# Retention's output projection in a two-layer trunk: another order of the seven Strassen products, other places for sums and splits

## The chip, the cores and the metric

The kernel runs on one core of a Trainium2 chip. The metric is the device time of one execution in microseconds (us). The engines are named as the profile names them: PE (TensorE matmul), PEld (its weight load), DVE (VectorE), ACT (ScalarE), POOL (GpSimd), SP (SyncE, which issues most DMAs). Before the change three runs gave 1338.38, 1340.61 and 1341.14 us, median 1340.61.

## The reference

Two layers, each x + f(x): a retention layer (4 heads, keys of 256, values of 512, chunks of 128 tokens, a recurrent state), then sliding-window attention. The prompt has 1024 tokens and 8 more tokens are decoded. All is float32. What the change touches is the end of the retention layer:

```python
o, S = retention_scan(q, k, v, S0)                 # (B, L, 4 heads, 512)
o = rmsnorm(o, g_out.reshape(RET_HEADS, RET_DV)).reshape(B, L, RET_V)   # 2048 wide
o = o * jax.nn.silu(gate)
return x + o @ w_out, S.astype(S0.dtype)           # w_out is 2048 x 1024
```

## The kernel before, in words

A float32 product is made as three passes over rounded parts: with x = xh + xl and w = wh + wl (h the rounded value, l what is left), PE adds wh·xh, wh·xl and wl·xh. So each operand needs a copy that rounds (ACT, the "hi" part) and a subtraction (DVE or POOL, the "lo" part).

**Retention steps.** 32 steps, one for each head and chunk. Each leaves a gated output block. Blocks of the first half of the 2048 rows (part a of the projection) stay in SBUF as `hold`; those of the second half (part b) go to DRAM, `osc`.

**Strassen.** Part a and part b each multiply 1024 tokens by a 1024 x 1024 half of w_out, as 2 x 2 blocks. Seven products replace eight: activations come as raw blocks (B11, B21, B22) or as sums of them (T1 to T4), weights as raw blocks (A11, A12, A22) or sums (S1 to S4, tiles `s`; `raw` is the loaded weight). A weight sum S2 is made from S1, and S4 from S2. Activation blocks are rounded to `oxh` by `ox_hi` (L881, ACT) and `oxl` by `ox_lo` (L885); the decoded tokens' two columns for each block are split by `dec_split` (L895, L896) and summed by `dec_sums` (L901). Sums of `hold` blocks are `sum_op` (L1052, DVE).

**Sets and slots.** A set is one part and one of four column groups q: sets 0 to 3 are part a, sets 4 to 7 part b. A set has seven products in two token halves t, 14 slots of 12 matmuls (L1127 to L1129). In part a the last four products also take the residual x by two transposes for each slot (L1132), from tiles `xr` that a DMA loads (L1180) and, for the last, POOL subtracts from one another (`res_diff`, L1183). Weights are summed on POOL (`w_sum`, L209 to L218) and split by `w_hi` (L238, ACT) and `w_lo` (L243, DVE).

The order is A11, S2, S1, A12, S3, S4, A22. Each product is written to one of three PSUM banks for each t or added to what stands there: A12 is added to the bank of A11, S4 to that of S1, and S3 and A22 to that of S2. Since the combination needs what stood in a bank between its products, the bank is read first (`o_evac`, L1148 to L1164: ACT for A11, and for A12 in part a; DVE else) into `evp`, `evx`, `evc`, `evw`. So A12 waits until A11's bank is read, and A22 until S3's is, with two products and one product between them.

**What sets the order.** A planner (`Table`) lists the slots with assumed times; `when(t, ...)` puts a piece of work before the slot that is due at t, `later(n, ...)` behind slot n. Each engine executes its instructions in the order in which they are written, so a late operand delays all that stands behind the instruction that waits for it.

**Part b's activations.** During sets 0 to 3 the raw blocks are loaded from DRAM into one ring of five tiles `ob` (L1112), summed (L1354, two sums of each group of four on DVE, two on POOL) and stored again. From set 3 on, all 28 blocks are loaded once more into the same ring and split into `oxh` and `oxl`, the lo parts alternately on DVE and POOL.

**Out of a set.** `out_a` (L1203) stores part a's result; `out_b` adds it to part b's (`pa_add` L1195, L1211), squares it for the next norm and stores it. In set 7 `a_split` (L1252, L1253) and `kvs_conv` (L1410, L1411) prepare attention's operands and weights.

Of the kernel before, what the change touches and what calls it, by code (L numbers as in the profile page):

```python
# [7 lines left out]
F32 = mybir.dt.float32  # L8
# [65 lines left out]
def _trunk(ctx, tc, nc, a):  # L74
# [129 lines left out]
    def w_sum(s, name, sub, part=0):  # L204
        sh = [128, 512 // s.fw, s.fw]
        wq, nb = (s.pool(), 1) if s.kind == "o" else (wq_, 2)
        if name == "S2" and part == 0:
            t = s.sum["S1", sub] = wq.tile(sh, F32, tag="s1", bufs=nb, name="s1")
            pool.tensor_tensor(t, quad(s, 1, 0, sub), quad(s, 1, 1, sub), ADD)  # L209
        elif name == "S2":  # L210
            t = s.sum["S2", sub] = wq.tile(sh, F32, tag="s2", bufs=nb, name="s2")
            pool.tensor_tensor(t, s.sum["S1", sub], quad(s, 0, 0, sub), SUB)  # L212
        elif name == "S3":
            t = s.sum["S3", sub] = wq.tile(sh, F32, tag="s1", bufs=nb, name="s3")
            pool.tensor_tensor(t, quad(s, 0, 0, sub), quad(s, 1, 0, sub), SUB)
# [4 lines left out]
    def wop_tile(s, sh, nm):  # L220
        if s.kind == "o":
            return s.pool().tile(sh, F32R, tag="wop", bufs=6, name=nm)
# [642 lines left out]
    ORD7 = (B11, T2, T1, B21, T3, B22, T4)  # L865
# [25 lines left out]
    def dec_split(x):  # L891
# [3 lines left out]
        dve.tensor_copy(h, src)  # L895
        dve.tensor_tensor(l, src, h.bitcast(F32), SUB)  # L896

    def dec_sums():
        a_, b_, c_, d_ = dec_blocks(0)
        for out, x, y in ((a_, c_, a_), (c_, d_, c_), (d_, d_, a_), (b_, b_, d_)):  # L900
            dve.tensor_tensor(out, x, y, SUB)  # L901
# [149 lines left out]
    def sum_op(out, x, y):  # L1051
        dve.tensor_tensor(out, x, y, SUB)  # L1052
# [14 lines left out]
    plan_builds(6, 30)  # L1067
# [40 lines left out]
    KEYS = (("c", 0, 0), ("w", 1, 1), ("x", 0, 1), ("p", 1, 0))  # L1108
# [29 lines left out]
    def o_raw(s, j):  # L1138
        t = s.pool().tile([128, 4, 256], F32, tag="raw", bufs=2, name="raw")
# [4 lines left out]
    def o_evac(s, j, t):  # L1144
        c = s.c
        b0, b1, b2 = [s.bk[i, t][:, 0:258] if (i, t) in s.bk else None for i in range(3)]
        if j == 0:
            act(o_out(s, "p", t), b0, AF.Copy)  # L1148
        elif j == 1:
            dve.tensor_tensor(c["p", t], b1, c["p", t], ADD)  # L1150
        elif j == 2:
            dve.tensor_tensor(o_out(s, "x", t), b2, c["p", t], ADD)
        elif j == 3 and s.part == 0:
            act(o_out(s, "c", t), b0, AF.Copy)
        elif j == 3:
            dve.tensor_tensor(o_out(s, "c", t), b0, s.pa["c"][:, t, :], ADD)
        elif j == 4 and s.part and s.q:
            dve.tensor_tensor(c["w", t], b1, c["w", t], ADD)  # L1158
        elif j == 4:
            dve.tensor_tensor(o_out(s, "w", t), b1, c["x", t], ADD)  # L1160
        elif j == 5:
            dve.tensor_tensor(c["x", t], b2, c["x", t], ADD)
        else:
            dve.tensor_tensor(c["p", t], b1, c["p", t], ADD)  # L1164
# [12 lines left out]
    def res_load(s, key, i, par):  # L1177
        r = s.res[key] = sg[0].tile([128, 4, 128], F32, tag="xr", bufs=4, name="xr")
# [11 lines left out]
    def pa_add(s, key):  # L1190
        if key == "w":
            for t in range(2):
                o_out(s, "w", t)
        src = both(s, "x" if key == "w" else key)
        pool.tensor_tensor(both(s, key), src, s.pa[key], ADD)  # L1195
# [10 lines left out]
    def out_b(s, key, i, par):  # L1206
# [3 lines left out]
        if key != "c" and s.q == 0:  # L1210
            dve.tensor_tensor(r, r, s.pa[key], ADD)  # L1211
# [4 lines left out]
        if s.q == 3:  # L1216
# [5 lines left out]
            dve.scalar_tensor_tensor(alo, pr, gk, af, MUL, SUB)  # L1222
        if s.q == 0 and key in "cw":
# [5 lines left out]
        for t in range(2):  # L1229
            soon_dma(xscr[ft, :, 512 * t:512 * t + 512].rearrange("p (c r x) -> r p c x", r=2, x=128)[par], pr[:, t])  # L1230
# [11 lines left out]
    def a_load(k, par, tile_=lambda: ob[0].tile([128, 4, 128], F32, tag="ob", bufs=5, name="ar")):  # L1242
# [21 lines left out]
    def o_slot(s, j, t):  # L1264
        name, x, b, first = SEQ7[j]
# [1230 lines left out]
```

## Time and profile before

| | us |
|---|---|
| runs (median of three) | 1340.61 |
| profiled execution | 1336.95 |
| its span, first to last instruction | 1335.1 |
| retention steps | 551.5 to 706.6 |
| projection, sets 0 to 7 | 708.29 to 894.20 |
| PE busy in the projection's 185.91 us | 175.70 |
| DVE, ACT, POOL busy there | 127.36, 76.35, 130.96 |

A line of the trace has a start, a duration, the engine and line, the operation with output and input tiles, and in brackets the idle time before it with what ended it. A line of waits has engine, line, what it waited for, us in total, number of times, the longest. A line of a table of windows has the window and its length, then for each engine its busy time and number of instructions, TensorE's granted clock, the DMA engines' busy share and GB/s. A PE that is busy in a window may still be slow inside a slot; a slot's cost is read from start to start.

### The profile page before, as it was taken

What the parts mean: (1) busy time and instruction counts of PE and PEld (TensorE: products, weight loads), DVE (VectorE), ACT (ScalarE), POOL (GpSimd) and SP (SyncE); (2) the same over time, 40 slices, a digit from 0 to 9 for tenths busy, and PEclk for the clock granted to TensorE, in tenths of its full rate; (3) what the DMA queues carried; (4) which work ended last, traced back from release to release, by engine and by line L of the source; (5) the groups of instructions that cost most, each with busy time, mean ns of one, the idle gap of its engine ahead of it and who ended that gap; (6) DMA issues with size and microseconds to landing.
All of it is one profiled execution on the core that took longest, in us unless ns stands there. A gap on an engine that the chain in (4) does not pass through costs nothing.

```text
span 1335.1 us, 26918 instructions
## 1 busy us (share of the span) xinstructions
PE 1276.3 (96%) x9613; PEld 1231.1 (92%) x9613; DVE 852.9 (64%) x1684; ACT 709.0 (53%) x1739; POOL 852.9 (64%) x1011
## 2 busy tenths in 40 slices
PE   6999999999999999899899998988999999999998
PEld 6999999999999999787689998988999999998998
DVE  6953655665666554487987567576677777778421
ACT  5522545555555664376664244345576676766321
POOL 6643555656556665378797576875688787878510
PEclk9999999999999999999999998999999999999999
DMA  6313867586667762545777987653131110113532
GB/s 223 103 50 109 241 190 237 171 257 202 189 209 215 224 194 89 190 159 188 211 232 218 324 273 243 176 171 96 45 93 51 33 60 25 46 29 108 186 95 77
DMA packets 217306, 207.93 MB, mean 156 GB/s; under 512 B 19348, under 2 KB 185228, under 8 KB 217156
## 3 DMA queue, kind: packets, MB, share of 16 engines
q1 hardware_dynamic: 188848, 178.27, 43.0%
q10 hardware_dynamic: 28324, 27.94, 6.7%
q8 instruction: 76, 1.25, 0.4%
q14 instruction: 58, 0.48, 0.1%
HBM read 137.10 MB, written 70.09 MB: 155 GB/s over the span
## 4 chain that ended last, share of the span: by engine, by line
PE 67%; POOL 11%; DVE 10%; DMA 6%; issue 4%; ACT 2%; SPq 0%; POOLq 0%; ACTq 0%; DVEq 0%
PE b L359 7%; PE b L361 7%; PE b L360 7%; PE pj L1593 5%; PE pj L1594 5%; PE pj L1595 5%; PE b L353 4%; PE b L354 4%; PE b L352 4%; PE tr L104 3%; DMA ob<-osc 2%; DVE Sl L1006 1%; POOL s L2038 1%; POOL pw L1578 1%; PE S L1129 1%
## 5 line engine op out<-in xcount | busy, mean ns | idle before, releaser
L359 PE MATMUL b<-xh,woh 128*128 128x258 f32 x784 | 222.1, 283 | 0.0
L361 PE MATMUL b<-xh,wol 128*128 128x258 f32 x784 | 221.5, 283 | 0.0
L360 PE MATMUL b<-xl,woh 128*128 128x258 f32 x784 | 221.3, 282 | 0.0
L1593 PE MATMUL pj<-A_hi,pw 128*128 128x384 f32 (+1 forms) x512 | 172.5, 337 | 0.0
L1594 PE MATMUL pj<-A_lo,pw 128*128 128x384 f32 (+1 forms) x512 | 163.9, 320 | 1.0 <-POOL A_lo L1840 0.7
L1595 PE MATMUL pj<-A_hi,pw 128*128 128x384 f32 (+1 forms) x512 | 163.8, 320 | 0.0
L359 PEld LDWEIGHTS b<-xh,woh 128*128 128x128 f32 x784 | 148.1, 189 | 1.2
L360 PEld LDWEIGHTS b<-xl,woh 128*128 128x128 f32 x784 | 148.6, 190 | 0.0
L361 PEld LDWEIGHTS b<-xh,wol 128*128 128x128 f32 x784 | 148.0, 189 | 0.0
L353 PE MATMUL b<-wol,xh 128*128 128x256 f32 x448 | 126.7, 283 | 2.5 <-DVE wol L243 2.5
L352 PE MATMUL b<-woh,xh 128*128 128x256 f32 x448 | 126.5, 282 | 0.0
L354 PE MATMUL b<-woh,xl 128*128 128x256 f32 x448 | 126.3, 282 | 0.0
L243 DVE TENSOR_TENSOR wol<-s,woh 128x512 fp32r<-128x512 f32 x120 | 102.0, 855 | 18.3 <-ACT woh L238 17.6
L238 ACT ACTIVATE woh<-s 128x512 fp32r<-128x512 f32 x120 | 73.9, 623 | 71.2 <-POOL s L212 32.4
L301 POOL TENSOR_TENSOR yl<-yd,yh 128x256 fp32r<-128x256 f32 x64 | 57.0, 890 | 79.3 <-PE od L308 42.6
L243 POOL TENSOR_TENSOR wol<-raw,woh 128x512 fp32r<-128x512 f32 x52 | 68.9, 1332 | 52.1 <-ACT woh L238 51.2
L1594 PEld LDWEIGHTS pj<-A_lo,pw 128*128 128x128 f32 x512 | 96.6, 189 | 1.6 <-POOL A_lo L1840 1.0
L1127 PE MATMUL S<-oxh,woh 128*128 128x258 f32 x320 | 94.2, 294 | 3.8 <-DVE evw L1158 2.8
L1593 PEld LDWEIGHTS pj<-A_hi,pw 128*128 128x128 f32 x512 | 96.4, 188 | 0.6 <-issue 0.3
L1595 PEld LDWEIGHTS pj<-A_hi,pw 128*128 128x128 f32 x512 | 96.2, 188 | 0.0
L1129 PE MATMUL S<-oxh,wol 128*128 128x258 f32 x320 | 92.0, 287 | 3.8 <-DVE wol L243 3.8
L1128 PE MATMUL S<-oxl,woh 128*128 128x258 f32 x320 | 91.5, 286 | 0.0
(423 smaller groups left out, 4064.2 us busy)
## 6 DMA issues: line engine op xcount, KB each, us to landing
raw<-in_w_in_ret_dram ACTq DMA_DIRECT2D x44, 512.0 KB
st<-in_state_ret_dram SPq DMA_DIRECT2D x64, 256.0 KB
out_dram<-st SPq DMA_DIRECT2D x64, 256.0 KB
vb<-vscr SPq DMA_DIRECT2D x64, 128.0 KB
evp<-qks SPq DMA_DIRECT2D x32, 256.0 KB
evw<-gsc SPq DMA_DIRECT2D x32, 256.0 KB
raw<-in_w_out_ret_dram SPq DMA_DIRECT2D x16, 512.0 KB
wr<-in_w_in_swa_dram SPq DMA_DIRECT2D x14, 512.0 KB
```

The costliest lines, as they stand in the source:

```text
L243: eng.tensor_tensor(lo, src_of(s, name, sub), hi.bitcast(F32), SUB)
L352: mm(dst, xh, wh, start=a and i == 0, stop=False, skip_group_check=True)
L353: mm(dst, xh, wl, start=False, stop=False, skip_group_check=True)
L354: mm(dst, xl, wh, start=False, stop=z, skip_group_check=True)
L359: mm(dst, wh, xh, start=a, stop=False, **sg)
L360: mm(dst, wh, xl, start=False, stop=False, **sg)
L361: mm(dst, wl, xh, start=False, stop=z, **sg)
L1127: mm(dst, wh, xh, start=a, stop=False, **sg_k)
L1129: mm(dst, wl, xh, start=False, stop=z, **sg_k)
L1593: mm(ps, wh, AH(k)[:, t0:t1], start=first and k == ks[0], stop=False)
L1594: mm(ps, wh, AL(k)[:, t0:t1], start=False, stop=False)
L1595: mm(ps, wl, AH(k)[:, t0:t1], start=False, stop=last and k == ks[-1])
```

## The change

The order of products becomes A11, A12, S4, S2, S1, S3, A22, with other banks: S4 has a bank of its own, S1 takes the one of A11 and A12, and A22 is added to S3's directly after it. What was evicted as one sum for `evx` is done in two steps, the later one after S1. Sum S4 moves from POOL to DVE, in place in raw A12. The weights have one ring of six split tiles instead of two such rings used in turn, and are prepared 4.5 us before use (S4 3.9) instead of 6.5. Residual tiles are loaded 11 us ahead instead of 8 and subtracted 7 us ahead instead of 4.5.

In the retention steps, the decoded columns' work moves from steps 15 to 22 to steps 1 to 10 (its copies from DVE to ACT). Of the sixteen sums of `hold`, the last group's four and the `b` sums of all groups move behind the last step, with T1's four splits and T2's last one; of those that stay, two of three go to POOL. The projection's first slot is issued to PE ahead of the transposes of the output of the last step but one, which came before it.

For part b, the raw blocks B11 and B21 stay in SBUF from their one load (tiles `oa`, `ob`, four each, and `ot`, five, in place of one ring of five), so that 20 blocks instead of 28 are loaded for splitting. Of its sums three of four go to DVE; of its 28 splits 16 go to DVE and 12 to POOL. Squares and stores of a set's result come some slots later, and `kvs_conv` 7 us and more later.

```diff
-    ORD7 = (B11, T2, T1, B21, T3, B22, T4)
+    SEQO = (("A11", B11, 0, True), ("A12", B21, 0, False), ("S4", B22, 1, True), ("S2", T2, 2, True),
+            ("S1", T1, 0, True), ("S3", T3, 2, True), ("A22", T4, 2, False))
...
     def w_sum(s, name, sub, part=0):
+            elif name == "S4":
+                t = quad(s, 0, 1, sub)
+                dve.tensor_tensor(t, t, s.sum["S2", sub], SUB)
...
-        dve.tensor_copy(h, src)
+        act(h, src, AF.Copy)
...
-            seq_ += [(sum_op, a_, c_, a_), (sum_op, c_, d_, c_), (ox_hi, T1, j, a_), (ox_lo, T1, j, a_),
-                     (sum_op, d_, d_, a_), (ox_hi, T2, j, d_), (ox_lo, T2, j, d_), (sum_op, b_, b_, d_)]
+            if j < 3:
+                seq_ += [(sub, a_, c_, a_), (sub, c_, d_, c_), (sub, d_, d_, a_, dve)]
+            if j < 3:
+                seq_ += [(ox_hi, T2, j, d_), (ox_lo, T2, j, d_)]
...
-            th_ = max(tf - 6.5, floor + (3.2 if name != "A11" else 0.0))
+            th = first[name] - (3.9 if name == "S4" else 4.5) - (6.0 if n_ == 0 and name in ("A11", "A12", "S4") else 0.0)
...
+    a3, c3, d3 = hold[0, 6], hold[0, 7], hold[1, 7]
+    for t_, x in ((-2.0, (a3, c3, a3)), (-0.7, (c3, d3, c3)), (0.6, (d3, d3, a3))):
+        tb.when(t_, sub, *x)
+    for j in range(3, 4):
+        tb.when(2.0, late_build, T2, j, dve)
+    for j in range(4):
+        tb.when(2.7 + 1.5 * j, lambda j=j: sub(hold[1, 2 * j], hold[1, 2 * j], hold[1, 2 * j + 1]))
+        tb.when(2.4 + 0.9 * j, late_build, T1, j, (dve, pool)[j % 2])
+        tb.when(6.2 + 0.8 * j, late_build, T3, j, (dve, pool)[j % 2])
+        tb.when(9.2 + 1.1 * j, late_build, T4, j, (dve, pool)[j % 2])
...
+        for i_, (x, n_, tag) in enumerate(((B11, 0, "oa"), ("c", 2, "ot"), ("d", 3, "ot"), (B21, 1, "ob"))):
+            tb.when(t_ + 0.05 * i_, b_load, x, n_, j, tag)
+        tb.when(t_ + 5.5, b_sums, j)
+        tb.when(t3 + 5.0 + 0.8 * j, b_load, B22, 3, j, "ot")
     m = 0.0
     for n_, x in enumerate(ORD7):
         for j in range(4):
-            m = max(m + 1.1, osets[3].t0 + 2.95 * n_ + 3.0)
-            tb.when(m - 6.0, xb_load, x, j)
-            tb.when(m, xb_build, x, j)
+            m = max(m + 1.15, t3 + 2.95 * n_ + 3.0)
+            tb.when(m, xb_build, x, j, (dve, dve, pool, dve, pool, dve, pool)[(4 * n_ + j) % 7])
+            y = {B11: (T2, 5, "oa"), B21: (T1, 4, "ob"), B22: (T3, 6, "ot"), T2: (T4, 7, "oa")}.get(x)
+            if y:
+                tb.when(m + 2.0, b_load, y[0], y[1], j, y[2])
...
+        if i == len(steps) - 1:
+            tb.pe()
         at_step(b_tr, i - 1)
```

POOL's program at the opening of the projection, from the last steps' `bss` (the norm's exponent) to the first weight sum of set 1, before the change:

```order
L120 TENSOR_TENSOR bss<-bss,mhalf 128x1 x2
L215 TENSOR_TENSOR s_9883<-raw 128x512
L885 TENSOR_TENSOR oxl<-hold,oxh 128x4x128
L218 TENSOR_TENSOR s_9777<-raw,s_9777 128x512
L885 TENSOR_TENSOR oxl<-hold,oxh 128x4x128 x3
L1203 TENSOR_TENSOR evc<-evc,xd 128x2x2
L209 TENSOR_TENSOR s_10100<-raw 128x512
```

The same stretch of POOL's program now, between the last `bss` and the residual's subtraction and the sum behind it (L1068 is a sum of `hold`, L901 a split, L216 the sum S3):

```order
L120 TENSOR_TENSOR bss<-bss,mhalf 128x1
L1068 TENSOR_TENSOR hold<-hold 128x512 x2
L901 TENSOR_TENSOR oxl<-hold,oxh 128x4x128
L1068 TENSOR_TENSOR hold<-hold 128x512
L901 TENSOR_TENSOR oxl<-hold,oxh 128x4x128
L1068 TENSOR_TENSOR hold<-hold 128x512
L216 TENSOR_TENSOR s_9979<-raw 128x512
L901 TENSOR_TENSOR oxl<-hold,oxh 128x4x128
L1068 TENSOR_TENSOR hold<-hold 128x512
L1218 TENSOR_TENSOR evc<-evc,xd 128x2x2
L901 TENSOR_TENSOR oxl<-hold,oxh 128x4x128 x2
L1201 TENSOR_TENSOR xr<-xr 128x512
```

One more split of T4 and set 1's first sums follow. Ahead of the first `bss` of this piece stand two more sums of `hold`.

DVE's program about the start of set 4, before, where part b's splits (`oxl<-ob`) stand among the weight splits of A11's followers:

```order
L885 TENSOR_TENSOR oxl<-ob,oxh 128x4x128
L1164 TENSOR_TENSOR evp<-S,evp 128x258
L885 TENSOR_TENSOR oxl<-ob,oxh 128x4x128
L243 TENSOR_TENSOR wol<-s_11007,woh 128x512
L885 TENSOR_TENSOR oxl<-ob,oxh 128x4x128
L243 TENSOR_TENSOR wol<-raw,woh 128x512
L1150 TENSOR_TENSOR evp<-S,evp 128x258
```

The corresponding piece now, from set 3's last evictions (L1181) to set 4's A12 (L1171); L212 is the sum S4:

```order
L1181 TENSOR_TENSOR evp<-po,evp 128x258
L256 TENSOR_TENSOR wol<-raw,woh 128x512
L212 TENSOR_TENSOR raw<-raw,s_11027 128x4x128
L1181 TENSOR_TENSOR evp<-po,evp 128x258
L901 TENSOR_TENSOR oxl<-ob,oxh 128x4x130 x2
L256 TENSOR_TENSOR wol<-raw,woh 128x512
L1171 TENSOR_TENSOR evc<-S,pa 128x258
L901 TENSOR_TENSOR oxl<-ob,oxh 128x4x130
L256 TENSOR_TENSOR wol<-s_11027,woh 128x512
```

The splits of `ob` still stand between the weight splits; the S4 sum has joined them. What the splits read is now mostly loaded long before.

DVE's program in set 7, up to S3's evictions (evw<-S,evw, L1158), before:

```order
L243 TENSOR_TENSOR wol<-s_11883,woh 128x512
L1156 TENSOR_TENSOR evc<-S,pa 128x258
L1253 SCALAR_TENSOR_TENSOR A_lo<-ar,gcol,A_hi 128x4x128
L1156 TENSOR_TENSOR evc<-S,pa 128x258
L1222 SCALAR_TENSOR_TENSOR A_lo<-evc,gcol,A_hi 128x4x128
L243 TENSOR_TENSOR wol<-raw,woh 128x512
L1158 TENSOR_TENSOR evw<-S,evw 128x258
```

And now, up to S3's evictions in their new form (evw<-po,evw, L1179); L1175 evicts S1, L1177 is the second step of evx:

```order
L1175 TENSOR_TENSOR evw<-S,evp 128x258
L1272 SCALAR_TENSOR_TENSOR A_lo<-ar,gcol,A_hi 128x4x128
L256 TENSOR_TENSOR wol<-raw,woh 128x512
L1177 TENSOR_TENSOR evx<-S,evw 128x258
L1175 TENSOR_TENSOR evw<-S,evp 128x258
L1272 SCALAR_TENSOR_TENSOR A_lo<-ar,gcol,A_hi 128x4x128
L1177 TENSOR_TENSOR evx<-S,evw 128x258
L1179 TENSOR_TENSOR evw<-po,evw 128x258 x2
```

Fewer wide instructions stand directly ahead of S3's evictions; the one A_lo that followed A12's evictions is further ahead.

More of the change, by code (lines that the diff above doesn't have):

```diff
@@ L1264, in o_slot @@
     def o_slot(s, j, t):
[L1265 removed]
+        name, x, b, first = SEQO[j]
         n = len(tb.slots)
[L1267 removed]
+        key = KEYS.get(name)
+        done = KEYS.get({"S1": "S4", "S4": None}.get(name, name))
+        res = s.part == 0 and key
         def pe():
@@ L1328, in open_b @@
+        if s.part == 0:
+            tb.when(first["A22"] - 7.0, res_diff, s)
+        elif s.q:
+            tb.later(s.n0 + 11, pa_add, s, "p", pool)
     def open_b():
```

228 lines of the change are left out of this document (118 added, 110 removed).

## The prediction

> **What bounds the kernel now.** I read the page first, to see which engine carries the time.
>
> ```profile
> PE 1276.3 (96%) x9613; PEld 1231.1 (92%) x9613; DVE 852.9 (64%) x1684; ACT 709.0 (53%) x1739; POOL 852.9 (64%) x1011
> ```
>
> PE does, so a change that leaves its matmuls alone can win only what PE loses. Where that is in the stages touched, I read from windows cut at the starts of the eight sets:
>
> ```profile
> core 0: us, PE busy (x) PEld busy (x) DVE busy (x) ACT busy (x) POOL busy (x), PEclk, DMA share, GB/s
> 708.29:731.54 23.25, 23.25 (x200) 23.03 (x198) 18.74 (x28) 10.78 (x23) 15.41 (x13) 1.00 0.78 236
> 731.54:754.37 22.83, 22.37 (x188) 22.02 (x186) 12.78 (x21) 5.01 (x11) 13.50 (x14) 1.00 0.92 284
> 754.37:777.85 23.48, 22.41 (x188) 22.00 (x186) 12.36 (x21) 5.53 (x12) 13.64 (x13) 1.00 0.89 301
> 777.85:800.71 22.86, 22.20 (x188) 21.99 (x186) 17.50 (x22) 13.60 (x26) 15.60 (x13) 1.00 0.90 303
> 800.71:829.52 28.81, 23.81 (x172) 23.05 (x171) 20.83 (x29) 12.64 (x24) 20.82 (x18) 0.88 0.81 261
> 829.52:849.71 20.19, 20.19 (x170) 20.19 (x169) 11.78 (x21) 8.20 (x15) 14.33 (x14) 1.00 0.60 176
> 849.71:870.16 20.45, 20.43 (x170) 20.25 (x169) 13.48 (x22) 7.65 (x15) 19.15 (x19) 1.00 0.63 181
> 870.16:894.20 24.04, 21.05 (x172) 20.54 (x171) 19.90 (x24) 12.96 (x24) 18.51 (x16) 1.00 0.66 198
> ```
>
> Set 5 runs without a gap: 20.19 us for 14 slots, 1.44 a slot. That is the floor of a part-b set. Part a has two residual transposes more in eight of its slots; its floor is about 21.9, just under the 22.0 for which PEld was busy in each of sets 1 to 3, so that such a slot takes (21.9 − 6 x 1.44) / 8 = 1.66. Above the floor lie: set 0 1.3 (0.6 of it the last step's four transposes), sets 1 to 3 0.9, 1.5 and 0.9, set 4 8.6, sets 5 and 6 0.3 together, set 7 3.9. So 17.4 us in all, half of it in set 4. What ended the waits in set 4 is in the waits of 800.7 to 829.5:
>
> ```profile
> ACT oxh L881 <- DMA ob<-osc: 11.7, 8, 2.6
> DVE oxl L885 <- ACT oxh L881: 7.5, 4, 5.7
> PE S L1129 <- DVE wol L243: 3.8, 1, 3.8
> ```
>
> In set 4, ACT waits for the reloaded blocks of part b, DVE waits for ACT inside a split of theirs, and the weight split of A12 stands behind it. The granted clock fell to 0.88 with the gap. The same reading for the retention steps: windows of steps 3 to 10 and 15 to 23, then the price of what DVE has in some of them.
>
> ```profile
> 567.94:604.54 36.60, 36.60 (x203) 30.93 (x202) 30.15 (x68) 24.34 (x60) 29.62 (x35) 1.00 0.52 166
> 623.55:670.68 47.13, 39.48 (x216) 32.14 (x215) 40.83 (x90) 29.90 (x72) 36.58 (x41) 1.00 0.74 218
> ...
> L895 DVE CAST oxh<-gdec x5: 182/425/429, 637.9 to 664.9; 128x16 fp32r<-128x16 f32 x5
> L896 DVE TENSOR_TENSOR oxl<-gdec,oxh x5: 379/661/672, 638.3 to 665.3; 128x16 fp32r<-128x16 f32 x5
> L901 DVE TENSOR_TENSOR gdec<-gdec x4: 175/545/1015, 652.5 to 654.7; 128x16 f32<-128x16 f32 x4
> L1052 DVE TENSOR_TENSOR hold<-hold x16: 690/717/728, 594.3 to 697.7; 128x512 f32<-128x512 f32 x16
> ...
> PE tr L104 <- DVE on L1025: 11.6, 10, 2.2
> ```
>
> A step at PE's pace takes 36.60 / 8 = 4.575 us; nine steps of 15 to 23 take 47.13, which is 5.9 too much. The decoded columns' work lies there: 5 x 0.425 + 5 x 0.661 + 4 x 0.545 = 7.6 us on DVE. PE waits for DVE's `on`.
>
> **The change part by part.** The sum is made against the profiled execution, 1336.95, which lies 3.7 below the median of the runs, 1340.61; the same difference is then applied to the median.
>
> *Retention steps.* DVE loses 13 of 16 sums (13 x 0.717 = 9.3) and five casts (2.1, now on ACT); POOL gains six sums and loses five splits. The other 5.5 us of decoded work go to steps 4 to 10, where DVE has 30.15 busy in 36.60, so 0.8 free in a step; seven steps have 5.6. It fits, just. Best case: the 5.9 go, and 0.7 more of steps 11 to 14. Worst: nothing goes and 1.8 is added, since the work meets POOL's splits early and steps 16 and 17 wait for other reasons. I take half of the best, −3.3, for T2's rounding still waits for a sum in three steps; ends −6.6 and +1.8.
>
> *Opening and set 0.* These rows show PE's wait before the first slot, and what POOL and DVE instructions cost alone and beside each other:
>
> ```profile
> 707.91 0.63 PE L104 MATMUL tr<-ident,on 128*128 128x128 f32 x4 [0.46 <-DVE on L1025]
> ...
> 706.43 0.54 POOL L120 TENSOR_TENSOR bss<-bss,mhalf 128x1 f32<-128x1 f32 x1
> 711.76 1.29 POOL L215 TENSOR_TENSOR s<-raw 128x512 f32<-128x512 f32 x1 [1.56 <-DVE wol L243]
> 798.76 1.75 POOL L212 TENSOR_TENSOR s<-s,raw 128x512 f32<-128x512 f32 x1
> ...
> 710.90 0.68 DVE L243 TENSOR_TENSOR wol<-s,woh 128x512 fp32r<-128x512 f32 x1
> 712.05 1.55 DVE L243 TENSOR_TENSOR wol<-raw,woh 128x512 fp32r<-128x512 f32 x1 [0.46 <-ACT woh L238]
> ```
>
> With the first slot ahead of those transposes it starts at about 707.3, when the last step's matmuls end, 1.0 earlier. But POOL now has, behind the `bss` that ends at 706.97, seven sums, six splits and one weight sum, 14 x 1.28 = 17.9 us, then small ones of 2.2 (a `bss` 0.54, the residual's subtraction 1.28, and the tiny `evc`, taken as 0.4). Beside a wide DVE instruction it took 1.75, so 0.47 more; DVE has about 15 such in this stretch, of which I let 11 collide: 5.2. POOL ends T4's last split at 706.97 + 25.3 = 732.3. A22's second slot, the last of the set, would be due at 707.3 + 0.6 (the transposes) + 21.9 − 1.66 = 728.1. So PE waits 4.2, and set 1 starts at 732.3 + 1.66 = 734.0, against 731.54: +2.4, taken as +2.3. Ends: +0.5 if half of POOL's collisions and its order cost nothing, +5 if also ACT's roundings queue, whose evictions stand behind them.
>
> The 712.05 row shows DVE held for 0.87 us while POOL worked, so each delays the other. The Trainium skill, "SBUF — State Buffer", section on the two separate sides, says that GpSimd and a two-input VectorE operation share a port pair under an exclusive lock, and that the loser blocks for the other's whole instruction. By that rule all 15 DVE instructions would cost POOL their full 0.68, 10.2 instead of 5.2, so this term would be +7.3; the 1.75 row bears out two thirds of it.
>
> *Sets 1 to 3.* Two rows of the waits of 731 to 801, and one of DVE's timeline:
>
> ```profile
> PEld S L1132 <- POOL xr L1183: 2.1, 2, 1.2
> ...
> 768.20 0.70 DVE L1354 TENSOR_TENSOR ob<-ob 128x520 f32<-128x520 f32 x1 [2.89 <-DMA ob<-osc]
> ```
>
> The residual's subtraction comes 2.5 us earlier, more than PE's waits for it: −2.3 with the loads. New is that A22 follows S3 in its bank: S3's first eviction now has one slot, 1.66, instead of three. In DVE's program one of part b's sums stands ahead of it in set 2 alone; a load late by 2.89, as here, would cost about 1.5 there, and I take a third, +0.5. Sum −1.8; ends −3.3 (all of the loss) and +6, two a set.
>
> *Set 4.* 8 of 28 loads go, and 16 of the others start as soon as a split has freed a tile, by the planner's times about 12 us ahead of use instead of 6. ACT's 11.7 us of waiting for them should go, and with it DVE's wait of 5.7. Against it, splits and weight work of DVE and POOL still collide; S4's sum comes to DVE as well (0.7). I leave 2 of 8.6: −6.6; ends −8.6 and 0.
>
> *Sets 5 and 6.* Nothing to win but 0.3. POOL's squares and additions come later and are behind nothing that PE reads. S3 to A22 is tighter here too: +0.5, ends 0 and +3.
>
> *Set 7 and the end.* A row of the waits of 870 to 900, and DVE's timeline at S3's eviction, for which A22 waits:
>
> ```profile
> PE S L1127 <- DVE evw L1158: 2.8, 1, 2.8
> ...
> 888.61 1.78 DVE L243 TENSOR_TENSOR wol<-raw,woh 128x512 fp32r<-128x512 f32 x1
> 890.31 0.41 DVE L1158 TENSOR_TENSOR evw<-S,evw 128x258 f32<-128x258 f32 x1
> ```
>
> S3's first slot ends about 870.16 + 9 x 1.45 = 883.3, its eviction starts at 890.31: 7 us late, behind splits like the 1.78 here, which is 0.68 alone, beside POOL's `kvs_conv` and additions. Now `kvs_conv` comes 7 us later and fewer wide instructions stand ahead of that eviction. Of 3.9 I take half, −2; ends −5 (part of the wait after the last slot too) and +3, if `kvs_conv` meets the last splits, and attention starts later.
>
> Everything else (smaller rings, later squares, later stores) I cost at nothing: it is covered by PE's 20 to 22 us a set, in which DVE is busy 12 to 13 in sets 1, 2, 5 and 6; if that cover goes, it shows as lateness of evictions, the first rival.
>
> Sum: −3.3 + 2.3 − 1.8 − 6.6 + 0.5 − 2 = −10.9. So 1326.1 for the profiled execution, 1329.7 against the median; I say 1330.
>
> **The rivals.**
>
> *Slower: a shorter distance inside the banks.* A12 follows A11, and A22 follows S3, with one slot of 1.44 to 1.66 for the eviction between. The old order hid late evictions. That they are late, two rows of ACT in set 4 show:
>
> ```profile
> 804.75 0.64 ACT L881 ACTIVATE oxh<-ob 128x520 fp32r<-128x520 f32 x1 [1.67 <-DMA ob<-osc]
> ...
> 807.16 0.37 ACT L1148 ACTIVATE evp<-S 128x258 f32<-128x258 f32 x1
> ```
>
> A11's first slot ended at 802.4, its eviction began 4.8 later; set 7's S3 had 7.0, less one slot 5.6. If such lateness stays in set 4 to 6 for A11 (3.3 past the slot, as much in set 5 as an estimate from this row, and 0.8 in set 6) and S3's in sets 1 to 4 is as in the 768.20 row (2.89 of waiting and 0.70 of the sum, less a slot of 1.66, so 1.9 a set and 7.7 in all), it costs 7.4 + 7.7 + 5.6 = 20.7, less the 0.5 counted: −10.9 + 20.2 = +9.3, 1350. It decides from 54% of that lateness on. For it: ACT still has roundings ahead of A11's eviction. Against: that row's wait ends with a DMA that the change takes away or starts earlier. Chance 0.25.
>
> *The change doesn't ease part b.* Loads were never the limit, the splits on DVE and POOL are; they grow no shorter. Then set 4's term is 0: −4.3, 1336. For it: DVE and POOL are each busy 20.8 of 28.8 us there. Against: ACT's wait of 11.7. Chance 0.13.
>
> *A heavy opening.* POOL and DVE exclude each other fully, so that each of DVE's 15 wide instructions holds POOL for 0.68: 10.2 instead of 5.2, hence −5.9, 1335. For it is DVE's 1.55; against it, POOL's 1.75 is not 1.28 + 0.68 = 1.96. Chance 0.12. This is the case that the rule of the Trainium skill named above would give.
>
> **How the numbers follow.** Forecast 0.50, then 0.25, 0.13, 0.12. Combining the terms' ends by squares gives 5.5 below and 13 above the sum: 1324 to 1343; the first rival's middle stretches the upper end to 1346, and the lower goes to 1322. Within 0.2% (2.7 us), about what a measurement here can tell from no change, is 1337.9 to 1343.3. Faster: 0.49 of the forecast, nearly all of the third and half of the second rival, 0.69; the same 0.08; slower 0.23, nearly all from the first.
>
> **What would show it.** Set windows: set 4 at 20 to 23 us, sets 1 to 3 near 22, set 0 at 26 with PE waiting for POOL's oxl in A22, set 7 at 22. Steps 15 to 23 near 43 us, 4 to 10 still 4.6 each. ACT no longer waits for ob<-osc in set 4. Wrong would be PE waits on ACT's evp in A12 and on DVE's evw in A22 of every set, or PE waiting for `on` in steps 4 to 10.

## The result, and the profile after

The changed kernel took 1329.45 us in the median of five runs (1327.19 to 1331.17), the kernel before 1338.38 in five runs beside it (1334.88 to 1341.14). The ratio is 0.9932, 95% interval 0.9909 to 0.9955: faster by 0.45% to 0.91%. The forecast was 1330 in a range of 1322 to 1346, so time and sign came out as forecast. Not all the terms of the sum did.

The profiled execution took 1329.56 us against 1336.95, 7.4 less. Its page shows the same PE work, and its windows, cut at the starts of the sets as before, where the time went:

```profile
PE 1275.8 (96%) x9613; PEld 1231.6 (93%) x9613; DVE 861.4 (65%) x1682; ACT 708.6 (53%) x1746; POOL 847.8 (64%) x1006
```

```profile
702.58:729.40 26.82, 24.58 (x202) 23.50 (x200) 22.67 (x30) 13.64 (x30) 24.97 (x19) 1.00 0.69 201
729.40:751.36 21.96, 21.96 (x187) 21.96 (x186) 15.05 (x26) 5.63 (x11) 9.88 (x10) 1.00 0.95 306
751.36:773.45 22.09, 22.09 (x187) 22.00 (x186) 14.90 (x24) 5.65 (x11) 13.41 (x13) 1.00 0.92 312
773.45:795.42 21.97, 21.97 (x187) 21.97 (x186) 17.80 (x27) 15.31 (x29) 13.08 (x12) 1.00 0.96 320
795.42:819.81 24.39, 21.57 (x172) 20.60 (x171) 24.04 (x30) 10.52 (x20) 20.45 (x17) 1.00 0.67 198
819.81:839.97 20.16, 20.16 (x170) 20.16 (x169) 13.83 (x23) 7.07 (x13) 12.67 (x12) 1.00 0.58 171
839.97:860.54 20.57, 20.46 (x171) 20.25 (x169) 16.17 (x20) 7.07 (x13) 15.35 (x15) 1.00 0.68 203
860.54:886.70 26.16, 22.06 (x172) 21.89 (x171) 24.65 (x29) 14.50 (x26) 20.55 (x18) 0.93 0.59 161
```

Sets 1, 2, 3, 5 and 6 now run within 0.4 us of their floors. Three sets don't: set 0 (4.9 above, 0.6 of it the transposes), set 4 (4.2) and set 7 (6.0). In set 4 DVE is busy 24.04 of 24.39 us, in set 7 24.65 of 26.16, in set 0 POOL 24.97 of 26.82. What ended the waits is in their tables of waits, two rows each, in the order set 0, 4, 7:

```profile
ACT oxh L897 <- POOL hold L1068: 4.1, 2, 2.2
PE po L1146 <- DVE wol L256: 1.1, 2, 0.8
...
PE po L1146 <- DVE wol L256: 1.9, 2, 1.5
PEld S L1144 <- ACT evp L1167: 0.7, 1, 0.7
...
PE po L1144 <- DVE evw L1179: 4.1, 1, 4.1
ACT A_hi L1236 <- DVE evx L1210: 7.2, 1, 7.2
```

The retention steps, windows of steps 3 to 10 and 15 to 23:

```profile
568.07:605.40 37.33, 36.81 (x204) 30.93 (x202) 30.84 (x74) 25.69 (x66) 28.79 (x36) 1.00 0.63 164
623.99:666.08 42.09, 39.14 (x217) 32.32 (x215) 30.15 (x68) 28.40 (x69) 34.37 (x42) 1.00 0.73 241
```

The late steps are 5.0 us shorter and the early ones 0.7 longer, which is one step, step 10. (Steps 16 and 17, where ACT waits 4.2 us for stores of the state, vary from run to run by 2.4 us, and 1.3 of the 5.0 are theirs; the table of runs below leaves them out.)

At a matmul of attention that began at 937 us before, the changed kernel is ahead by 10.2 us. It keeps that to 1240 us and loses 2.6 in the last projection, which the change doesn't touch. There nearly the same stretch had another granted clock, 1.00 before (first row) and 0.89 after (the second block: its window, then a row of its waits):

```profile
1278.00:1290.00 12.00, 12.00 (x83) 11.93 (x82) 3.37 (x13) 2.28 (x6) 0.00 (x0) 1.00 0.45 133
```

```profile
1268.90:1282.40 13.50, 13.50 (x84) 13.43 (x83) 3.37 (x13) 2.23 (x6) 0.00 (x0) 0.89 0.41 118
DVE sq L2265 <- DMA xr<-xscr: 10.5, 3, 5.5
```

So about 1.5 of the 2.6 go with the clock. Another 1.0 is in two waits of PE for DVE, which grew from 0.59 to 1.22 and from 0.71 to 1.08. DVE waited there for the residual's load, 10.5 us in three waits, 6.2 in two before; that the load is the cause was not tried. Of the runs below, the eight with a lowered clock at that place lose 2.2 to 4.6 us there against the kernel before, the four without it 0.7 to 1.7. Why the clock falls in some of them is open.

### The profile page after: what moved, and what is told of

Same layout as the page of the kernel before. It is cut to its first block, busy times and chain, and to the rows that moved or that the text cites. A ratio compares the mean times of both kernels' runs of the same rounds, so it can differ in the third digit from the quotient of the medians.

```text
span 1327.7 us, 26879 instructions
## 1 busy us (share of the span) xinstructions
PE 1275.8 (96%) x9613; PEld 1231.6 (93%) x9613; DVE 861.4 (65%) x1682; ACT 708.6 (53%) x1746; POOL 847.8 (64%) x1006
## 5 line engine op out<-in xcount | busy, mean ns | idle before, releaser
L256 DVE TENSOR_TENSOR wol<-s,woh 128x512 fp32r<-128x512 f32 x112 | 97.4, 876 | 10.1 <-ACT woh L251 9.5
L251 ACT ACTIVATE woh<-s 128x512 fp32r<-128x512 f32 x112 | 69.3, 623 | 43.6 <-POOL s L216 11.1
L2077 POOL TENSOR_TENSOR s<-s,sm 128x512 f32<-128x512 f32 x64 | 66.6, 1040 | 34.4 <-DVE sm L2076 33.7
L366 PEld LDWEIGHTS b<-wol,xh 128*128 128x128 f32 x448 | 85.2, 190 | 2.7 <-DVE wol L256 2.7
L251 ACT ACTIVATE woh<-raw 128x512 fp32r<-128x512 f32 x106 | 65.1, 624 | 42.1 <-PE po L1145 25.4
```

The costliest lines, as they stand in the source:

```text
L251: act(s.op[name, sub][0], src_of(s, name, sub), AF.Copy)
L256: eng.tensor_tensor(lo, src_of(s, name, sub), hi.bitcast(F32), SUB)
L366: mm(dst, xh, wl, start=False, stop=False, skip_group_check=True)
L2077: nc.gpsimd.tensor_tensor(u.st[:, :, 0:256], u.st[:, :, 0:256], u.sm.unsqueeze(2).broadcast_to([128, 2, 256]), ALU.mult)
```

## The experiments

Theories at the start. *Shared time*: DVE and POOL hold each other up, and sets 0, 4 and 7 are filled by the sum of both engines' work. *Own work*: DVE alone is too full there. *The bank*: S3 to A22 and A11 to A12 stand too close. For the retention steps: the *decoded columns' work*, or the *sums of hold*.

Lengths in us, read from first matmul to first matmul in each run's trace, one trace a run. "Steps" are steps 3 to 30 without 16 and 17; "opening" goes from the last step's first matmul to set 1; set 7 goes to the end of its last matmul; "to attention" from the first matmul behind set 7 to the one that began at 960 us before. In brackets stands TensorE's granted clock in set 7, and behind set 7 where it was under 1.00.

| run | steps | opening | sets 1–3 | set 3 + 4 | set 7 | to attention | time (runs) |
|---|---|---|---|---|---|---|---|
| before | 125.7 | 27.8 | 69.2 | 51.7 | 24.0 (1.00) | 66.2 | 1338.38 (5) |
| changed | 122.2 | 30.4 | 66.0 | 46.4 | 26.2 (0.93) | 63.5 | 1329.45 (5) |
| splits of part b on DVE | 121.4 | 30.4 | 68.7 | 45.4 | 26.0 (0.93) | 63.2 | 1328.47 (4) |
| opening on DVE | 121.2 | 31.2 | 66.2 | 46.4 | 27.0 (0.88) | 63.4 | 1328.40 (4) |
| decoded work late | 124.5 | 30.4 | 66.7 | 46.7 | 26.1 (0.93) | 63.4 | 1330.38 (4) |
| steps' sums on DVE | 121.3 | 30.4 | 66.1 | 46.4 | 26.2 (0.93) | 63.2 | 1332.37 (5) |
| bank for set 7's A22 | 122.5 | 30.4 | 66.7 | 46.4 | 23.0 (1.00) | 67.8 (0.97) | 1329.43 (3) |
| kvs_conv on DVE | 122.2 | 30.4 | 66.7 | 46.5 | 27.3 (0.87) | 63.4 | 1329.96 (3) |
| T2's last split later | 122.2 | 30.2 | 66.4 | 46.4 | 26.0 (0.93) | 63.5 | 1327.55 (4) |
| set 4's splits on DVE | 122.1 | 30.4 | 66.7 | 44.9 | 26.1 (0.93) | 63.2 | 1327.25 (2) |
| and S4 rounded later | 122.7 | 30.4 | 66.0 | 45.3 | 27.0 (0.87) | 63.1 | 1326.37 (4) |
| and two splits out of set 7 | 121.9 | 30.4 | 66.0 | 45.4 | 26.4 (0.87) | 64.8 (0.97) | 1328.77 (6) |
| first slot back | 121.2 | 30.1 | 66.5 | 46.7 | 27.0 (0.88) | 63.5 | 1328.13 (3) |
| three b sums back | 128.5 | 29.4 | 66.6 | 47.0 | 26.9 (0.87) | 63.5 | 1333.75 (9) |

The times spread by 2 to 9 us within one kernel, so what follows is read from the stages. Where a run doesn't touch them, sets 1 to 3 differ by up to 0.7 us, sets 3 and 4 by up to 0.6, and the steps by up to 1.5 (121.2 to 122.7). Set 7, where untouched, took 26.0 to 26.2 at a granted clock of 0.93 and 26.9 to 27.0 at 0.87 or 0.88, so runs are compared there at the same clock. PE's wait at A22 was the same 4.1 in the changed kernel and in two of the latter.

**Part b's splits, all on DVE.**

```diff
-            tb.when(m, xb_build, x, j, (dve, dve, pool, dve, pool, dve, pool)[(4 * n_ + j) % 7])
+            tb.when(m, xb_build, x, j, dve)
```

> The changed kernel with all 28 lo splits of part b on DVE (16 there and 12 on POOL before). In the changed kernel sets 3 and 4 took 21.97 and 24.39 us, and DVE was busy 24.04 us of the 24.39, POOL 20.45. Theory 'shared time': DVE and POOL hold each other up, a split alone takes 0.69 on DVE and 1.28 on POOL, and what fills set 4 is the sum of both engines' lone times. Then 12 x (1.28 - 0.69) = 7.1 us of it go, and set 4 falls to 20.5 to 22 us, the time to about 1326.5. Rival 'DVE is full by its own work': 12 x 0.69 = 8.3 us more on a full engine, set 4 at 27 to 31 us, the time 1333 to 1336.

Set 4 took 21.50 us as the first theory said, although DVE got 12 splits of 0.68 more. Set 3 got longer, 23.9. (Set 2's 22.8 isn't the edit's: DVE's instructions are those of the changed kernel up to 779 us.) The windows of sets 3 and 4, then two of DVE's splits in a row, and a row of the waits of both sets, the one that took the gain away:

```profile
773.83:797.74 23.91, 22.43 (x188) 21.98 (x186) 21.16 (x35) 15.20 (x29) 10.17 (x10) 1.00 0.98 335
797.74:819.24 21.50, 20.50 (x172) 20.33 (x170) 21.02 (x35) 10.58 (x20) 5.61 (x6) 1.00 0.52 178
...
784.88 1.29 DVE L901 TENSOR_TENSOR oxl<-ob,oxh 128x512 fp32r<-128x512 f32 x2
...
PE po L1144 <- DVE evw L1179: 2.4, 2, 1.4
```

Two splits take 1.29 together while POOL stands idle. "Own work" falls. But with more splits in DVE's queue S3's eviction is late in sets 3 and 4, and A22 waits for it: the bank coupling is real where DVE lags by more than a slot.

**The same from set 4 on.**

```diff
-            tb.when(m, xb_build, x, j, (dve, dve, pool, dve, pool, dve, pool)[(4 * n_ + j) % 7])
+            tb.when(m, xb_build, x, j, dve if m > t3 + 19.0 else (dve, dve, pool, dve, pool, dve, pool)[(4 * n_ + j) % 7])
```

> The changed kernel with part b's lo splits as there (DVE and POOL) up to about set 4's start and on DVE alone from there on. All 28 on DVE gave sets 2 to 4 at 22.8, 23.9 and 21.5 against 22.1, 22.0 and 24.4: set 4 lost its waits for weight splits, and set 3 got a wait in A22 for S3's eviction. Theory 'shared time with an S3 to A22 wait where DVE lags': set 3 back at 22.0, set 4 at 21 to 22, so 2.5 to 3 us gained on the two. Rival 'the gain in set 4 was only work done earlier in set 3': set 4 at 23.5 to 24.5, no gain.

Set 3 is back at 21.98, set 4 at 22.95: 1.4 gained, half of what was expected. All products from S4 on ran without waits for weights; A12 lost 2.4, in the order PE, ACT:

```profile
801.07 0.38 PE L1144 MATMUL S<-oxh,woh 128*128 128x258 f32 x1 [1.67 <-ACT evp L1167]
...
799.59 0.63 ACT L251 ACTIVATE woh<-raw 128x512 fp32r<-128x512 f32 x1 [2.56 <-DVE raw L212]
800.65 0.37 ACT L1167 ACTIVATE evp<-S 128x258 f32<-128x258 f32 x1
```

ACT stood 2.56 us at the rounding of S4's weights, whose sum DVE had not made; the eviction of A11's second half stood behind it.

**And S4's rounding and split 1.5 us later in set 4.**

```diff
-            th = first[name] - (3.9 if name == "S4" else 4.5) - (6.0 if n_ == 0 and name in ("A11", "A12", "S4") else 0.0)
+            th = first[name] - (3.9 - 1.5 * (n_ == 4) if name == "S4" else 4.5) - (6.0 if n_ == 0 and name in ("A11", "A12", "S4") else 0.0)
```

> The run before with set 4's splits on DVE (set 4 at 22.95 us) and, in set 4 alone, the rounding of S4's weights 1.5 us later, so that on ACT it stands behind the eviction of A11's second half and no longer ahead of it (ACT waited 2.6 us there for DVE's S4 sum, A12's second half 1.7 us for the eviction). Theory 'A11 to A12 in one bank, with ACT held': set 4 falls to 20.8 to 21.5 us, and A12 has no wait for evp. Rival 'the wait moves': S4's split comes late by as much, set 4 stays above 22.3.

Set 4 took 23.35. A12's wait for evp went, and S4 waited 2.16 for its split on DVE instead: the rival. But the edit also moves that split. DVE now had four of part b's splits and an eviction between the sum S4 and it, three splits before, and began it 8.4 us after the set's first matmul instead of 7.2. So the order on ACT was not tried alone. In both runs the wait at the start of set 4 goes back to DVE's queue: the sum S4, which the change had moved there, and what stands behind it.

**The opening on DVE.** All seven sums and the six splits that POOL had:

```diff
-        tb.when(t_, sub, *x)
+        tb.when(t_, sub, *x, dve)
...
-        tb.when(2.7 + 1.5 * j, lambda j=j: sub(hold[1, 2 * j], hold[1, 2 * j], hold[1, 2 * j + 1]))
-        tb.when(2.4 + 0.9 * j, late_build, T1, j, (dve, pool)[j % 2])
+        tb.when(2.7 + 1.5 * j, lambda j=j: sub(hold[1, 2 * j], hold[1, 2 * j], hold[1, 2 * j + 1], dve))
+        tb.when(2.4 + 0.9 * j, late_build, T1, j, dve)
...
```

> The changed kernel with the opening's seven sums of hold and its six POOL splits of T1, T3 and T4 on DVE. Set 0 took 26.82 us there, DVE busy 22.67 and POOL 24.97 of it. Theory 'shared time': 13 x (1.28 - 0.69) = 7.7 us of shared time go, set 0 falls to about 23.5 us (21.9 and the last transposes would be 22.6), the time to about 1326. Rival 'own work': DVE gets 9 us more on 22.67, set 0 takes 29 to 32 us, the time 1332 to 1335. Third theory, on order: PE waited in A12 and S2 because evictions and splits on ACT and DVE stand behind sums on POOL; taking POOL out helps these by the 1.5 us that ACT's roundings waited for POOL's sums, set 0 about 25.

Set 0 took 27.6 us, 0.8 more, so all three missed. DVE's instructions were 0.68 each, and its share of the work ended earlier. But the sum S3, the one wide instruction that POOL still had there, met a dense row of them (POOL, then DVE in the same time):

```profile
716.48 5.22 POOL L216 TENSOR_TENSOR s<-raw 128x512 f32<-128x512 f32 x1 [9.10 <-DVE wol L256]
```

```profile
717.46 1.28 DVE L901 TENSOR_TENSOR oxl<-hold,oxh 128x512 fp32r<-128x512 f32 x2
718.66 0.68 DVE L256 TENSOR_TENSOR wol<-s,woh 128x512 fp32r<-128x512 f32 x1
719.26 1.28 DVE L901 TENSOR_TENSOR oxl<-hold,oxh 128x512 fp32r<-128x512 f32 x2
```

A sum of 1.29 took 5.22; DVE's row ended at 720.5, the sum 1.2 us later. S3's product waited 1.34 for it. A12, ahead of all this, lost 2.7 (2.2 in the changed kernel, the transposes' 0.6 included in both). Moving work to the faster engine is no gain if the other keeps one instruction that is needed soon.

**T2's last split later.** On ACT, its rounding waits for POOL's sum d and stood ahead of A11's second eviction.

```diff
-        tb.when(2.0, late_build, T2, j, dve)
+        tb.when(4.0, late_build, T2, j, dve)
```

> The changed kernel with T2's last split planned 2 us later, so that on ACT the eviction of A11's second half stands ahead of the rounding that waits for POOL's sum (ACT waited 1.9 us there, PE 0.83 in A12). Theory 'order on ACT': set 0 falls from 26.82 to about 25.8, the wait for evp in A12 goes, the waits for weight splits in S2 and S3 may grow by part of it. Rival 'set 0 is filled by DVE's and POOL's shared time': the wait moves to S2, S3 or A22, and set 0 stays at 26.5 to 27.

Set 0 took 26.66. A12 was 1.1 us shorter, S2 0.95 longer: it waited 1.79 for its weight split instead of 0.83. The rival.

**First slot back behind the transposes.**

```diff
-        if i == len(steps) - 1:
-            tb.pe()
         at_step(b_tr, i - 1)
...
+    tb.pe()
     others(len(steps))
```

> The changed kernel with the projection's first slot again behind the transposes of the last step but one. Theory 'the early slot gains its microsecond': the projection starts 4.6 us after the last step's first matmul instead of 3.55, and as set 0 is held up later by waits for DVE, ACT and POOL, 0.3 to 1 us of it arrives at set 1. Rival 'set 0 is bound by its splits anyway': set 1 starts at the same distance from the last step (30.6 us) within 0.3.

The projection began 4.77 us after the last step's first matmul instead of 3.54, and set 1 began 30.1 after it instead of 30.4. The early slot's 1.2 us are lost again within set 0: the rival. In this run, in the one above and in the changed kernel set 1 begins 1.6 us behind the end of POOL's last split of T4, which came 28.5, 28.6 and 28.7 us after the last step's first matmul.

**Three b sums back in the steps.**

```diff
-                seq_ += [(ox_hi, T2, j, d_), (ox_lo, T2, j, d_)]
+                seq_ += [(ox_hi, T2, j, d_), (ox_lo, T2, j, d_), (sub, b_, b_, d_)]
...
-        tb.when(2.7 + 1.5 * j, lambda j=j: sub(hold[1, 2 * j], hold[1, 2 * j], hold[1, 2 * j + 1]))
+        if j == 3:
+            tb.when(2.7 + 1.5 * j, lambda j=j: sub(hold[1, 2 * j], hold[1, 2 * j], hold[1, 2 * j + 1]))
```

> The changed kernel with three of the four b sums of hold back in the retention steps (on POOL, behind T2's splits), so that POOL has 3 sums fewer in the opening. Set 0 took 26.82 us there, and set 1 began 30.4 us after the last step's first matmul. Theory 'the opening is filled by POOL's and DVE's work': 3 x 1.3 to 1.75 = 4 to 5 us of it go, set 0 at 22.7 to 24, the steps lose 0.5 to 1.5 where POOL gets a second item. Rival 'the opening's waits are a chain at its start (transposes, on, the eviction of A11 and the first weight splits)': set 0 at 25.8 to 26.8, and the steps lose as much.

The opening gained 1.0, not 4 to 5. Set 0's 25.9 lies in the rival's range, but the last wait of the set was for POOL, its last split of T4, in A22's second slot:

```profile
730.47 1.09 POOL L901 TENSOR_TENSOR oxl<-hold,oxh 128x512 fp32r<-128x512 f32 x1
...
731.61 0.39 PE L1145 MATMUL po<-oxl,woh 128*128 128x258 f32 x1 [0.39 <-POOL oxl L901]
```

It ended 27.8 us after the last step's first matmul, only 0.9 earlier than in the changed kernel: with three sums fewer POOL stood waiting for ACT's roundings instead, 2.06, 1.65 and 1.33 us.

The steps lost 6.3, far more than either said. The list of the steps' work is spread evenly over them, so three more items also moved the others, and twice DVE's sum d now stood waiting for POOL's, with the norm's `bss` behind it (a row of the waits, then DVE and POOL in step 11):

```profile
DVE hold L1068 <- POOL hold L1068: 4.9, 2, 2.5
...
604.29 0.69 DVE L1068 TENSOR_TENSOR hold<-hold 128x512 f32<-128x512 f32 x1 [2.48 <-POOL hold L1068]
...
607.07 0.73 POOL L120 TENSOR_TENSOR bss<-bss,mhalf 128x1 f32<-128x1 f32 x1 [2.81 <-DVE bss L1033]
```

The two steps, 11 and 18, were 3.4 and 1.7 us longer than in the changed kernel, step 11 at a granted clock of 0.86 instead of 1.00. So most of the 6.3 goes with that order, and the price of the b sums in themselves stays open.

**Decoded columns' work late again.**

```diff
-        if 3 <= i < 7:
-            dec_store(i - 3)
-        if 4 <= i < 7:
-            dec_split((B11, B21, B22)[i - 4])
-        if i in (7, 8):
-            dec_sums(i - 7)
-        if i in (9, 10):
-            dec_split((T1, T2)[i - 9])
+        if i in (17, 18, 19):
+            dec_split((B11, B21, B22)[i - 17])
+            dec_store(i - 17)
+        if i == 20:
+            dec_sums(0)
+            dec_sums(1)
+            dec_store(3)
+        if i in (21, 22):
+            dec_split((T1, T2)[i - 21])
```

> The changed kernel with the decoded columns' products, splits, sums and stores back in steps 15 to 22 (the rounding stays on ACT). The last retention step started 4.7 us earlier in the changed kernel than in the old one. Theory 'decoded work': this was its cost on DVE in steps 17 to 23, so that 3 to 4.5 us come back, the time about 1333. Rival 'sums of hold': the gain comes from the 13 sums that DVE lost, then 0 to 1 us come back, the time 1329 to 1331.

The steps lost 2.3 of the 3.5 us that the change had gained in them, most in step 21 (6.03 instead of 4.58). It is under the 3 to 4.5 expected, but the casts stay on ACT in this run. The place of the decoded work is the larger part of the gain; the 1.2 left for casts and sums together is no more than the steps' spread.

**The steps' sums on DVE again.**

```diff
-                seq_ += [(sub, a_, c_, a_), (sub, c_, d_, c_), (sub, d_, d_, a_, dve)]
+                seq_ += [(sub, a_, c_, a_, dve), (sub, c_, d_, c_, dve), (sub, d_, d_, a_, dve)]
```

> The changed kernel with the six sums of hold that it does on POOL within the retention steps on DVE again. Theory 'decoded work' (the gain of 4.7 us in the steps is that of the decoded columns): no change, within 0.7 us in the steps. Rival 'sums of hold': 6 x 0.72 = 4.3 us on DVE, 1.5 to 2.5 us lost in the steps. Theory 'shared time': POOL's item of 1.28 goes and DVE's 0.72 comes, so steps 10, 17, 24 and 29, which ran over by 0.5 to 0.8 with POOL at over 5 us of work, go back to 4.58: 1 to 2 us gained, the time about 1328.

The steps were 0.9 us shorter (step 10 4.75 instead of 5.29, step 24 4.56 instead of 5.07), about the spread between runs. For these six sums "sums of hold" falls; their move to POOL was no part of the gain. The seven that left the steps altogether were put back on DVE in no run.

**A bank of its own for set 7's A22.**

```diff
             dve.tensor_tensor(c["w", t], b2, c["w", t], ADD)
+            if (s.part, s.q) == (1, 3):
+                dve.tensor_tensor(c["p", t], b2, c["p", t], ADD)
         elif name == "A22":
-            dve.tensor_tensor(c["p", t], b2, c["p", t], ADD)
+            dve.tensor_tensor(c["p", t], b1 if (s.part, s.q) == (1, 3) else b2, c["p", t], ADD)
...
+        if name == "A22" and (s.part, s.q) == (1, 3):
+            b, first = 1, True
```

> The changed kernel with a bank of its own for set 7's A22 (that of S4, read two slots after S1), so that it no longer waits for S3's eviction; that eviction becomes two DVE instructions for each half. In the changed kernel set 7 took 26.15 us, 5.9 over its floor, and A22 waited 4.1 us for DVE's evw of S3. Theory 'the bank': 2 to 4 us come back in set 7, and the time falls by as much. Rival 'DVE is full there, the bank only shows it': set 7 gets shorter by 1 to 2.5 us, but the next wait, behind A22's eviction on DVE, grows by as much or more, and the time stays within 1 us.

Set 7 took 23.0, 3.1 less, and the way to attention 67.8 instead of 63.5, 4.3 more: 1.2 lost in sum. A22 still waited for DVE, now for the reading of S4's bank. PE's wait there, DVE's last eviction and the next norm's first instruction, in the changed kernel and in this one:

```profile
882.07 0.36 PE L1144 MATMUL po<-oxh,woh 128*128 128x258 f32 x1 [4.10 <-DVE evw L1179]
...
887.59 0.75 DVE L1181 TENSOR_TENSOR evp<-po,evp 128x258 f32<-128x258 f32 x2
...
893.20 0.16 DVE L1657 TENSOR_SCALAR r<-tr 128x4 f32<-128x4 f32 x1 [0.43 <-PE tr L1651]
```

```profile
881.63 0.36 PE L1144 MATMUL S<-oxh,woh 128*128 128x258 f32 x1 [2.45 <-DVE evx L1177]
...
890.22 0.75 DVE L1183 TENSOR_TENSOR evp<-S,evp 128x258 f32<-128x258 f32 x2
...
895.68 0.16 DVE L1661 TENSOR_SCALAR r<-tr 128x4 f32<-128x4 f32 x1 [0.32 <-PE tr L1655]
```

Counted from set 7's first matmul (860.54 and 861.74), PE was done 3.1 us earlier, and DVE began that norm 1.3 later. Of the 3.1, 1.6 is the wait; most of the rest is the granted clock, 1.00 in set 7 instead of 0.93, while it was 0.97 instead of 1.00 behind it. One of the two added instructions waited 1.07 for POOL, so the price of 1.2 isn't clean; that no gain arrives is: the clock was 1.00 from set 7's end to 896.9, and DVE's norm was late before that. The bank shows where DVE is late; it isn't the cause.

**kvs_conv's lo parts on DVE.**

```diff
-        pool.tensor_tensor(lo, raw, hi.bitcast(F32), SUB)
+        dve.tensor_tensor(lo, raw, hi.bitcast(F32), SUB)
```

> The changed kernel with the four lo parts of kvs_conv on DVE instead of POOL. Set 7 took 26.15 us with DVE busy 24.65 and POOL 20.55. Theory 'shared time': 4 x (1.28 - 0.69) = 2.4 us of shared time go, set 7 at 24 to 25.5. Rival 'own work': 4 x 0.69 = 2.8 us more on a full DVE, set 7 at 28 to 29.

Set 7 took 27.3, between the two. In four other runs with set 7 untouched and the same granted clock, 0.87 or 0.88, it took 26.9 to 27.0, so the edit itself made about 0.3: too little for either theory.

**Two splits out of set 7** (on top of the run with S4 later):

```diff
-        tb.when(e7 + 15.6 + 2.0 * k, a_split, k, 0)
...
-        for k in ((), (2, 3), (4, 5))[n] if n < 3 else ():
+        for k in ((), (0, 1, 2), (3, 4, 5))[n] if n < 3 else ():
```

> The same, and two of the eight splits that prepare attention's operands in set 7 (a_split of the other parity, first two) moved behind the stage. Set 7 took 26.1 us with DVE busy 24.7. Theory 'DVE is full in set 7': two A_lo of 0.7 to 1.8 us go from DVE's queue there, set 7 at 23.5 to 25, and the start of attention is 1 to 2 us earlier; the time 1324 to 1326. Rival 'the bank of S3 and A22 alone sets it, by the order of its instructions': the two stood behind S3's evictions or close to them, set 7 at 25.5 or more, no gain.

Set 7 took 26.4 instead of 27.0 at the same granted clock, 0.87. S3's eviction began 20.4 us after the set's first matmul instead of 21.0, and A22 waited 3.5 instead of 4.1. That is a half microsecond where the theory wanted 1 to 2.5; the set's length fits the rival. The way to attention took 1.7 longer. PE waited 1.86 there for one of the moved splits, but its waits there in sum stayed at 3.3; what grew is its busy time, 61.4 instead of 59.7, at a clock of 0.97 instead of 1.00. What the moved splits cost in themselves can't be told from that.

No run was faster than the changed kernel beyond the spread: the two with set 4's splits on DVE, 1327.25 and 1326.37, have ratios of 0.9897 (0.9856 to 0.9937) and 0.9911 (0.9884 to 0.9938) against 0.9932 (0.9909 to 0.9955). No run puts back part b's loads, the residual's loads or the order of the products: what each of them gave is read from the waits that went, and was not tried.

## Why the prediction was right, term by term

The sum said −10.9 by the profiled execution; up to attention it is −10.2, and 2.6 were lost again at the end, which no term held. No term was made for the granted clock either, which fell in set 4 before and falls in set 7 now.

| term | predicted | measured |
|---|---|---|
| retention steps | −3.3 | −4.7 (−3.5 without steps 16 and 17) |
| opening and set 0 | +2.3 | +2.5 |
| sets 1 to 3 | −1.8 | −3.1 |
| set 4 | −6.6 | −4.4 |
| sets 5 and 6 | +0.5 | +0.1 |
| set 7 and the end | −2 | +2.1 in set 7, −2.7 behind it |

*Retention steps:* right in size and, by the run with the decoded work late, in its main cause. The place where PE's loss of 5.9 was read is the place that recovered.

*Opening:* the number was right, and so was the instruction named for the set's end, POOL's last split of T4. From the `bss` that ends at 702.5 to that split POOL took 25.2 us, against 25.3 reckoned, and set 1 began 1.6 us behind it. Wrong was where PE would lose its time. I put 4.2 us of waiting on A22's second slot. All of A22 lost 0.6, and the eviction on DVE that its second slot waited for ended within 0.1 us of POOL's split:

```profile
726.20 1.54 POOL L901 TENSOR_TENSOR oxl<-hold,oxh 128x512 fp32r<-128x512 f32 x1
...
727.71 0.39 PE L1144 MATMUL po<-oxh,woh 128*128 128x258 f32 x1 [0.32 <-DVE evw L1179]
```

The rest was lost on the way, in A12 (2.2 with the transposes), S2 (1.2), S3 (0.4) and A11 (0.4): first ACT, held by POOL's sum ahead of an eviction, then the weight splits on DVE. No term held these. That they replaced the predicted wait almost to the microsecond, so that PE's chain and POOL's ended together, was luck. The runs that ease the early waits (T2's split later, the first slot back) don't move the end by more than 0.3; with three sums fewer POOL's split still ends last and the gain is 1.0; with POOL's sums and splits on DVE other waits take its place, −0.8. And the 1.0 us for the first slot was no gain: set 1 doesn't start earlier for it.

*Sets 1 to 3:* nearly the best end. The loads for the residual and for part b's sums were early enough, and the new distance from S3 to A22 cost nothing there, because S3's eviction was hardly ever a slot late. In eight of the runs it was later in set 2, where one of part b's sums stands ahead of it, and set 2 took 22.4 to 22.8 instead of 22.1: about the 0.5 that was priced.

*Set 4:* the step that was mis-sized is "I leave 2 of 8.6". ACT's 11.7 us of waiting for loads went, as said. What was left is 4.2, waits for DVE's weight splits and for an eviction on ACT. With POOL's part of the splits on DVE all of set 4's waits for weights went, 2.9 us, at the price of 1.9 in set 3; with set 4's part alone 1.4 went, and most of what remained was the wait behind the sum S4. So the second rival, that the splits and not the loads are the limit, held for a part of the 4.2. And the 8.6 were not all waits. Before, PE stood idle for 5.0 us of set 4, and behind the longest wait, 3.84, its matmuls began 0.215 us apart instead of 0.12, at half the clock:

```profile
814.50:821.30 6.80, 5.68 (x26) 5.68 (x27) 6.61 (x10) 3.91 (x8) 6.18 (x4) 0.50 0.92 293
```

For these 26 matmuls that is about 2.5 us, as an estimate from the two intervals. The clock is 1.00 in set 4 in the changed kernel and in every other run here, so more than half of the 4.4 gained goes with the clock; that the longest wait had brought it down is likely from the order in time, but was not tried.

*Set 7:* the sign of the first half was wrong. S3's eviction is late as before, and A22, now directly behind it, waits 4.1 instead of 2.8, with a granted clock of 0.93 instead of 1.00: the first rival, at one of the places named for it. It costs nothing in the time: what attention waits for came 2.7 us sooner after set 7's end, and when the bank let PE finish 3.1 us earlier, nothing of it arrived. The rival failed in sets 4 to 6 in the main because A11's eviction was on time there; in set 4 it was late by 0.7.

*POOL and DVE beside each other:* the Trainium skill, "SBUF — State Buffer", section "SBUF: two separate sides", says that whichever starts first, a VectorE operation with two SBUF inputs or a GpSimd operation that reads SBUF, gets the shared port pair for the whole instruction, and that the other fully blocks. The runs agree that the two hold each other up: splits of 0.68 take 1.78 beside POOL, and 0.68 again with POOL quiet. The 5.22 us of POOL's sum go beyond a wait for one instruction of the other engine: they fit a sum that was passed over by a whole row of them. The rival built on full exclusion gave +7.3 for the opening; measured was +2.5.

## What to carry to other kernels

When DVE and POOL both work on SBUF, count an engine's queue by what stands ahead of the instruction that PE waits for, and not by the busy time of either: here taking work from POOL gave between −0.8 and +1.0 us in the opening, against 4 to 8 reckoned from busy times. An engine with less to do can end hardly sooner, because it then waits for others, as POOL did for ACT. A gain at the start of a stage (an earlier slot, a shorter chain) arrives only if that stage's own limit moves with it; check it at the next stage's start. And an evenly spread list of background work moves all its items when one is added, so that a new wait can arise far from the edit. Before a stage's length is compared between two runs, its granted clock is to be compared: here about 0.9 us of set 7's differences between runs came and went with it.

## What the runs showed of the hardware that was not expected

A POOL sum of 1.29 us took 5.22 beside an unbroken row of two-input DVE instructions, and ended 1.2 us after that row. Beside single ones, POOL's took 1.75 and DVE's 1.78. In a set with a long stall the granted clock fell (0.88 in set 4 before, with a wait of 3.84; 0.93 in set 7 after, with one of 4.10), and it fell to 0.89 in the last projection of the changed kernel's profile, behind waits of 1.22 and 1.08, which come without a fall in other runs. In set 7 before a wait of 2.80 left it at 1.00, while in step 11 of the run with three b sums back one of 2.23 came with 0.86. What decides is open.
